# RWKV chain: state, value and right-side products with 128 weight columns, issued as two column tiles of 64

## The chip, the cores and the metric

The kernel runs on one NeuronCore of a Trainium2 chip (trn2). The metric is the device time of one execution in microseconds (us), as the median of several runs. Times of instructions, waits and the granted clock of TensorE come from one profiled execution of the kernel before the change.

Words used below: PE is TensorE's matmul stream, PEld its weight loads, DVE VectorE, ACT ScalarE, POOL GpSimd, SP the queue that issues most DMAs. A *record* is one matmul entry of the trace; each float32 matmul call of the program shows up as two records, each with its own weight load. A *tile* of the array, as in `128*64`, is the number of its rows and columns that a matmul uses.

## The reference, cut to what matters

One serving step of a two-layer hybrid model over 640 tokens (512 latent, 128 context). One of four parallel branches is an RWKV-7 time mixing with 8 heads of width 64, run forward and backward. The change touches only the scan of this branch:

```python
def rwkv7_scan(r, decay, k, v, kk, a, s0, reverse):
    def step(s, inp):
        r_t, w_t, k_t, v_t, kk_t, a_t = inp
        s_kk = jnp.einsum('bhij,bhj->bhi', s, kk_t)
        s = (s * w_t[:, :, None, :] - s_kk[..., None] * (kk_t * a_t)[:, :, None, :]
             + v_t[..., None] * k_t[:, :, None, :])
        return s, jnp.einsum('bhij,bhj->bhi', s, r_t)
    xs = tuple(jnp.moveaxis(t, 1, 0) for t in (r, decay, k, v, kk, a))
    s_fin, out = lax.scan(step, s0.astype(F32), xs, reverse=reverse)
    return jnp.moveaxis(out, 0, 1), s_fin
```

The other branches (latent attention, a Mamba-2 scan, a gated linear recurrence) and the projections around them are the same before and after.

## The kernel before, in words

Each layer begins with a large input projection (76 blocks of 128 columns). Most of its blocks are not computed at once: they stand in a queue of generators (`enqueue`, `bg`), and every stage that follows takes pieces of that queue as filler between its own instructions. A filler piece is a run of `dense` matmuls (`mm3`, L246: weights 128x128, 320 moving columns, three products per block for a split float32). The RWKV stage (`rwkv`) comes first in each layer, then attention with the linear recurrence, then the Mamba-2 scan, then merge and output.

In the RWKV stage the scan is rewritten in chunks of 64 tokens. The 8 heads are handled as 4 pairs; a pair's two heads, e = 0 and 1, lie on partitions 0-63 and 64-127 (`hs`). `rw_chain` walks through 8 steps per pair; a step takes one chunk of each direction, and in steps 0, 1, 4 and 5 also a context chunk, so it has n = 2 or 3 units. The 2 layers, 4 pairs and 8 steps make 64 steps. All float32 products of a step go through `mm` (L541):

- **c** (out `ps`, weights `Q`, moving `S`): for each unit and head, 128 rows by 64 weight columns, out on the head's half of the partitions; ACT copies it, negated, to `xs` (L832).
- **y** from the state and the values (out `ps`, weights `Q`, moving `S`, L833-836): for each head and unit, 128 rows by 128 weight columns, 64 moving columns. The accumulation starts here.
- **W xs** (out `ps`, weights `W`, moving `xs`): 64 rows by 64 columns; DVE copies the result to `un` (L844).
- **y** from the right sides (out the same `ps`, weights `W`, moving `un`, L846-848): 64 rows by 128 weight columns, 64 moving columns. The accumulation ends here.

Half of each finished y is the next state (DVE, `S`, L852), the other half the output (`on`, ACT L856 and L862, DVE L858 and L864). POOL lays the next chunk's values into `S` beforehand (L809). `rwkv` takes the steps of a chain one by one and puts pieces of the next pair's preparation (`rw_half` with the matmuls `ps<-Q,BK`, `rw_solve`, `rw_values`) and of the filler queue (`self.bg(self.rb2)`) between them.

The order on each engine is not that of the code alone. The instructions are recorded in this interleaved order and then sorted per engine by a scheduler, on its own estimates of cost, before the program is fixed; each engine then takes its list strictly as it stands, with waits on semaphores between engines.

Of the kernel before, what the change touches and what calls it, by code (L numbers as in the profile page):

```python
# [169 lines left out]
class K:  # L170
# [624 lines left out]
    def rw_chain(self, l, p, H):  # L795

        nc, pr, V, hs = self.nc, H["pr"], H["V"], self.heads2()
        on = H["on"] = p.tile([128, T], F32, name="on", tag="on", bufs=2).rearrange("p (c i) -> p c i", i=64)

        def pairs(x, s):  # L800

            return x[:, s:8 - s:7 - 2 * s] if s < 4 else x[:, s:(6 - s if s < 7 else None):7 - 2 * s]

        def state(s):

            S = [p.tile([128, 3, 64], F32, name=f"S{e}", tag=f"S{e}", bufs=2) for e in range(2)]
            for e, r in enumerate(hs):
                o = hs[1 - e]
                nc.gpsimd.tensor_copy(S[e][o, 0:2], pairs(V[o], s))  # L809
                if s in ctx:  # L810
                    nc.gpsimd.tensor_copy(S[e][o, 2], V[o, ctx[s][1]])
                if s in (0, 4):
                    nc.gpsimd.memset(S[e][r, 2], 0.0)
            return S

        ctx = {0: (1, 9), 1: (1, 8), 4: (0, 8), 5: (0, 9)}
        S = state(0)
        for e, r in enumerate(hs):
            nc.sync.dma_start(out=S[e][r, 0:2], in_=self.a["st_rw"][l, pr, r])
        for s in range(8):  # L820
            chs = [(0, s), (1, 7 - s)] + ([ctx[s]] if s in ctx else [])
            n = len(chs)
            us = []
            for d, c in chs:
                hf, u = self.unit(d, c)
                us.append((*H["half"][hf], u))
            b = self.ps("c")
            for i, (Q, W, u) in enumerate(us):
                for e, r in enumerate(hs):
                    self.mm(b[r, 64 * i:64 * i + 64], Q[e][:, u, 0], S[e][:, i])  # L830
            xs = p.tile([128, 3, 64], F32, name="xs", tag="xs", bufs=2)
            nc.scalar.activation(out=xs[:, 0:n].rearrange("p i t -> p (i t)"), in_=b[:, 0:64 * n], func=AF.Copy, scale=-1.0)  # L832
            y = self.ps("y"), self.ps("y")  # L833
            for e in range(2):
                for i, (Q, W, u) in enumerate(us):
                    self.mm(y[e][:, 64 * i:64 * i + 64], Q[e][:, u, 1:3].rearrange("p x t -> p (x t)"), S[e][:, i], i == 0, False)
            S1 = state(s + 1) if s < 7 else [p.tile([128, 3, 64], F32, name=f"S{e}", tag=f"S{e}", bufs=2) for e in range(2)]
            yield
            b = self.ps("c")
            for i, (Q, W, u) in enumerate(us):  # L840
                for r in hs:
                    self.mm(b[r, 64 * i:64 * i + 64], W[r, u, 0], xs[r, i])
            un = p.tile([128, 3, 64], F32, name="un", tag="un", bufs=2)
            nc.vector.tensor_copy(un[:, 0:n].rearrange("p i t -> p (i t)"), b[:, 0:64 * n])  # L844
            yield
            for i, (Q, W, u) in enumerate(us):  # L846
                for e, r in enumerate(hs):
                    self.mm(y[e][:, 64 * i:64 * i + 64], W[r, u, 1:3].rearrange("p x t -> p (x t)"), un[r, i], False, i == n - 1)
            v = [x[:, 0:64 * n].rearrange("p (i t) -> p i t", t=64) for x in y]
            if s < 7:  # L850
                for e, r in enumerate(hs):
                    nc.vector.tensor_tensor(out=S1[e][r, 0:n], in0=v[e][r], in1=H["fac"][r, s, 0:n].unsqueeze(2).broadcast_to([64, n, 64]), op=ALU.mult)  # L852
            for e in range(2):
                o = hs[1 - e]
                if s < 4:
                    nc.scalar.copy(pairs(on[o], s), v[e][o, 0:2])  # L856
                else:
                    nc.vector.tensor_tensor(out=pairs(on[o], s), in0=v[e][o, 0:2], in1=pairs(on[o], s), op=ALU.add)  # L858
                if s in ctx:
                    oc = on[o, ctx[s][1]]  # L860
                    if s < 4:
                        nc.scalar.copy(oc, v[e][o, 2])  # L862
                    else:
                        nc.vector.tensor_tensor(out=oc, in0=v[e][o, 2], in1=oc, op=ALU.add)  # L864
            if s in (1, 5):
                for e, r in enumerate(hs):
                    nc.sync.dma_start(out=self.a["o_rw"][l, pr, r, chs[2][0]], in_=S1[e][r, 2])
            S = S1
            yield
# [861 lines left out]
```

## Time and profile before

| | before |
|---|---|
| median of 3 runs | 2509.02 us (2506.48 to 2519.65) |
| profiled execution, its time | 2516.37 us |
| span of the profile (first to last instruction) | 2514.5 us |
| PE busy | 2393.9 us, 95% of the span |
| PEld busy | 2106.9 us, 84% |
| DVE / ACT / POOL busy | 1711.5 / 1101.0 / 512.3 us |
| mean granted TensorE clock | 0.974 |
| matmul records | 19826 |

The profiled execution took 1.9 us more than its span, and 7.35 us more than the median of the runs. Matmuls are pipelined: a record of 0.27 us may start 0.06 us after the one before it. So the busy time of one group is far more than the PE time that it takes from others, and what a group costs is read from the starts of its records and not from their lengths.

### The profile page before, as it was taken

To read this page: it belongs to the slowest core of one execution; us is meant where nothing else is said; L and a number is where in the kernel's file an instruction comes from. 1 tells how busy PE (TensorE), PEld (TensorE's weight loads), DVE (VectorE), ACT (ScalarE), POOL (GpSimd) and SP (SyncE) were. 2 spreads that over 40 slices of the span, in tenths; PEclk is the share of its full clock that TensorE was granted. 3 is DMA by queue.
4 is the path that set the end of the run, shared out by engine and by line. 5 is a ranking of instruction groups with operands and counts; after the bars stand their busy time and mean duration, and the time that the engine had idled before them with its cause. 6 is when DMAs were issued, how large, how long until landed. Compare 5 with 4: busy or idle time off the path is not lost.

```text
span 2514.5 us, 49938 instructions
## 1 busy us (share of the span) xinstructions
PE 2393.9 (95%) x19826; PEld 2106.9 (84%) x19826; DVE 1711.5 (68%) x3749; ACT 1101.0 (44%) x2178; POOL 512.3 (20%) x723
## 2 busy tenths in 40 slices
PE   6999999999998989988999999999999999999999
PEld 4887877789987878977998978797999887898799
DVE  6575666664487777589765766675637777777883
ACT  3535243433344665453335362534224456555431
POOL 0322222121101230044103130312101013103420
PEclk9999999999999999999999999898999999999999
DMA  6443333433332213633633323132224222155354
GB/s 246 149 153 98 127 112 119 126 101 101 122 130 80 86 54 123 228 111 105 212 109 127 117 76 108 60 103 67 97 81 159 94 80 91 58 190 170 115 165 134
DMA packets 159192, 300.80 MB, mean 120 GB/s; under 512 B 59880, under 2 KB 70600, under 8 KB 158960
## 3 DMA queue, kind: packets, MB, share of 16 engines
q1 hardware_dynamic: 158528, 296.24, 35.4%
q8 instruction: 156, 2.56, 0.4%
q0 software_dynamic: 432, 1.38, 0.2%
q14 instruction: 76, 0.62, 0.1%
HBM read 221.17 MB, written 76.39 MB: 118 GB/s over the span
## 4 chain that ended last, share of the span: by engine, by line
PE 71%; DVE 15%; issue 4%; ACT 4%; DMA 4%; POOL 2%; SPq 0%; DVEq 0%; POOLq 0%; ACTq 0%
PE dn L246 40%; PE ps L541 11%; PE ps L246 6%; PE pd L1173 2%; PE ps L1124 2%; PE pd L1191 2%; PE ps L192 1%; PE ps L1438 1%; PE dn L457 1%; DVE wlo L234 1%; PE pd L1036 1%; DVE lt L1465 1%; DMA u<-zd 1%; PE ps L707 1%; DVE lm L1300 1%
## 5 line engine op out<-in xcount | busy, mean ns | idle before, releaser
L246 PE MATMUL dn<-hh,whi 128*128 128x320 f32 x2368 | 765.7, 323 | 2.8 <-DVE mod L470 1.3
L246 PE MATMUL dn<-hh,wlo 128*128 128x320 f32 x2368 | 748.8, 316 | 0.0
L246 PE MATMUL dn<-hl,whi 128*128 128x320 f32 x2368 | 748.0, 316 | 0.0
L246 PEld LDWEIGHTS dn<-hh,whi 128*128 128x128 f32 x2368 | 448.2, 189 | 30.8 <-issue 9.9
L246 PEld LDWEIGHTS dn<-hh,wlo 128*128 128x128 f32 x2368 | 447.5, 189 | 11.4 <-issue 6.7
L246 PEld LDWEIGHTS dn<-hl,whi 128*128 128x128 f32 x2368 | 448.3, 189 | 9.8 <-issue 5.1
L234 DVE TENSOR_TENSOR wlo<-raw,whi 128x1024 fp32r<-128x1024 f32 (+1 forms) x184 | 244.0, 1326 | 137.2 <-ACT whi L233 135.3
L233 ACT CAST whi<-raw 128x1024 fp32r<-128x1024 f32 (+1 forms) x184 | 191.7, 1042 | 272.9 <-PE dn L246 218.6
L541 PEld LDWEIGHTS ps<-S,Q 128*128 128x128 f32 (+1 forms) x1280 | 112.6, 173 | 33.0 <-issue 20.4
L809 POOL COPY S<-V 64x128 f32<-64x128 f32 x128 | 51.9, 406 | 425.9 <-PE ps L541 297.5
L246 PE MATMUL dn<-omh,whi 128*128 128x320 f32 x400 | 131.5, 331 | 4.1 <-DVE mx L1530 4.0
L541 PE MATMUL ps<-S,Q 128*128 128x64 f32 (+1 forms) x1280 | 130.7, 267 | 3.4 <-DVE S L852 2.3
L246 PE MATMUL dn<-oml,whi 128*128 128x320 f32 x400 | 126.8, 318 | 3.5 <-DVE oml L240 3.5
L670 DVE TENSOR_TENSOR Q<-ps,cpack 64x384 f32<-64x384 f32 x160 | 88.8, 555 | 58.5 <-ACT W L668 55.2
L246 PE MATMUL dn<-omh,wlo 128*128 128x320 f32 x400 | 126.9, 318 | 0.0
L541 PE MATMUL ps<-Q,BK 64*64 64x192 f32 x1280 | 101.1, 346 | 16.6 <-DVE Q L670 14.1
L668 ACT COPY W<-ps 64x384 f32<-64x384 f32 x160 | 75.6, 472 | 83.5 <-PE ps L541 81.2
L281 ACT COPY zst<-dn 128x320 f32<-128x320 f32 (+1 forms) x104 | 43.9, 422 | 132.4 <-PE dn L246 66.7
L541 PEld LDWEIGHTS ps<-Q,BK 64*64 64x64 f32 x1280 | 62.6, 136 | 41.3 <-DVE Q L670 20.6
L277 ACT ACTIVATE zst<-dn 128x320 f32<-128x320 f32 x128 | 55.3, 434 | 86.8 <-issue 47.9
L246 PEld LDWEIGHTS dn<-omh,whi 128*128 128x128 f32 x400 | 76.8, 193 | 18.5 <-issue 8.1
L753 DVE TENSOR_TENSOR X<-X,Lu 80x31 f32<-80x31 f32 (+15 forms) x248 | 85.6, 345 | 7.1 <-DMA Lu<-lud 1.1
(572 smaller groups left out, 4929.3 us busy)
## 6 DMA issues: line engine op xcount, KB each, us to landing
raw<-in_w_in_dram SPq DMA_DIRECT2D x152, 512.0 KB
zd<-zst SPq DMA_DIRECT2D x150, 320.0 KB
raw<-in_ada_w_dram SPq DMA_DIRECT2D x48, 512.0 KB
th<-zd SPq DMA_DIRECT2D x64, 320.0 KB
raw<-in_w_branch_dram SPq DMA_DIRECT2D x32, 512.0 KB
om<-od SPq DMA_DIRECT2D x32, 320.0 KB
u<-zd SPq DMA_DIRECT2D x26, 320.0 KB
raw<-in_w_out_dram SPq DMA_DIRECT2D x16, 512.0 KB
```

What stands on the lines that cost most here:

```text
L233: nc.scalar.copy(hi[:, 0:w], raw[:, 0:w])
L234: nc.vector.tensor_tensor(out=lo[:, 0:w], in0=raw[:, 0:w], in1=hi[:, 0:w].bitcast(F32), op=ALU.subtract)
L246: self.nc.tensor.matmul(o, w[wi], x[xi][:, sl], start=first and i == 0, stop=last and i == 2)
L277: nc.scalar.activation(out=u[:, tok], in_=t, func=AF.Tanh, scale=0.5)
L541: self.nc.tensor.matmul(o, x, y, start=start, stop=stop, skip_group_check=True)
L668: nc.scalar.copy(W[r, u:u + 2].rearrange("p u x t -> p (u x t)"), ps[e][r, 0:384])
L670: nc.vector.tensor_tensor(out=Q[e][o, u:u + 2].rearrange("p u x t -> p u (x t)"), in0=ps[e][o, 0:384].rearrange("p (u x) -> p u x", u=2), ...
L753: nc.vector.tensor_tensor(out=o, in0=X[0:nb, 0:m, k:k + 1].broadcast_to([nb, m, n]), in1=Lu[0:nb, k, k + 1:].unsqueeze(1).broadcast_to([nb ...
L809: nc.gpsimd.tensor_copy(S[e][o, 0:2], pairs(V[o], s))
L1124: nc.tensor.matmul(o[64 * x:64 * x + 64], vt[:, kt, hp * 128 + 64 * x:hp * 128 + 64 * x + 64], S[hp, t, x][:, j * 128:j * 128 + 128], star ...
L1173: nc.tensor.matmul(pd[:, b, 0:w], x[:, s], y[:, sl], start=i == 0, stop=i == 2)
L1191: nc.tensor.transpose(pd[:, i // 4, i % 4 * 128:i % 4 * 128 + 128], e[:, i * 128:i * 128 + 128], self.c["ident"])
```

## The change

Both y products are issued as two calls, one for each half of the weight columns (x = 0, 1), each writing its own half of the output partitions (`h`):

```diff
@@ -833,7 +833,8 @@
             y = self.ps("y"), self.ps("y")
             for e in range(2):
                 for i, (Q, W, u) in enumerate(us):
-                    self.mm(y[e][:, 64 * i:64 * i + 64], Q[e][:, u, 1:3].rearrange("p x t -> p (x t)"), S[e][:, i], i == 0, False)
+                    for x, h in enumerate(hs):
+                        self.mm(y[e][h, 64 * i:64 * i + 64], Q[e][:, u, 1 + x], S[e][:, i], i == 0, False)
             S1 = state(s + 1) if s < 7 else [p.tile([128, 3, 64], F32, name=f"S{e}", tag=f"S{e}", bufs=2) for e in range(2)]
             yield
             b = self.ps("c")
@@ -845,7 +846,8 @@
             yield
             for i, (Q, W, u) in enumerate(us):
                 for e, r in enumerate(hs):
-                    self.mm(y[e][:, 64 * i:64 * i + 64], W[r, u, 1:3].rearrange("p x t -> p (x t)"), un[r, i], False, i == n - 1)
+                    for x, h in enumerate(hs):
+                        self.mm(y[e][h, 64 * i:64 * i + 64], W[r, u, 1 + x], un[r, i], False, i == n - 1)
             v = [x[:, 0:64 * n].rearrange("p (i t) -> p i t", t=64) for x in y]
             if s < 7:
                 for e, r in enumerate(hs):
```

The tile of the array for the state products goes from 128*128 to 128*64 (as c has it), that of the right sides from 64*128 to 64*64 (as W xs has it). The number of calls of both doubles. Nothing else in the code differs, but the scheduler sorts the whole program anew, so fillers stand at other places too.

The PE's order before, in the second step of the first pair of layer 0 (`S_2108` and `S_2109` are the states of the two heads; 64x64 is the output of a c product, 128x64 that of a y product; L246 is filler):

```order
L541 MATMUL ps<-W,Z 32x32
L541 MATMUL ps<-un,W 128x64 x2
L541 MATMUL ps<-W,Z 32x32 x19
L541 MATMUL ps<-cpack,v 64x64 x20
L541 MATMUL ps<-un,W 128x64 x4
L707 MATMUL ps<-wl,lora 128x256
L707 MATMUL ps<-al,lora 128x256
L541 MATMUL ps<-S_2108,Q_822 64x64
```

The six products of the right sides (`un,W`) of the first step stand in two groups, between pieces of the next pair's preparation, and the next step's first c product follows.

The PE's order with the change at the place that follows (the states are now called `S_2114` and `S_2115`; y products are 64x64 as well, so the last two rows of six are y):

```order
L541 MATMUL ps<-un,W 64x64 x3
L707 MATMUL ps<-wl,lora 128x384
L541 MATMUL ps<-S_2114,Q_822 64x64
...
L541 MATMUL ps<-S_2115,Q_823 64x64
L541 MATMUL ps<-S_2114,Q_822 64x64
L541 MATMUL ps<-S_2115,Q_823 64x64
L541 MATMUL ps<-S_2114,Q_822 64x64
L541 MATMUL ps<-S_2115,Q_823 64x64
L457 MATMUL dn<-raw,csil 32x256
L541 MATMUL ps<-S_2114,Q_822 64x64 x6
L541 MATMUL ps<-S_2115,Q_823 64x64 x6
L541 MATMUL ps<-xs,W 64x64 x6
```

The right sides' last products have moved behind another piece of preparation. The y products have become twelve in place of six, and they stand where they stood, between the c products and W xs; no filler follows them here before W xs does.

The PE's order with the change in the third step, n = 2 (`Q,BK` are products of the next pair's preparation):

```order
L541 MATMUL ps<-S_2317,Q_822 64x64
L541 MATMUL ps<-S_2318,Q_823 64x64
L541 MATMUL ps<-S_2317,Q_822 64x64
L541 MATMUL ps<-S_2318,Q_823 64x64
L541 MATMUL ps<-S_2317,Q_822 64x64 x4
L246 MATMUL dn<-hh,whi 128x320
L246 MATMUL dn<-hl,whi 128x320
L246 MATMUL dn<-hh,wlo 128x320
L541 MATMUL ps<-S_2318,Q_823 64x64 x4
L541 MATMUL ps<-xs,W 64x64 x4
```

Here the four y products of head 0 follow the c products directly and those of head 1 stand behind one filler triple.

## Rows read from the trace of the kernel before

**Rows 1.** The page, parts 1 and 2: busy time, and 40 slices of the span.
```profile
PE 2393.9 (95%) x19826; PEld 2106.9 (84%) x19826; DVE 1711.5 (68%) x3749; ACT 1101.0 (44%) x2178; POOL 512.3 (20%) x723
...
PEclk9999999999999999999999999898999999999999
```

**Rows 2.** Busy time of each engine in four stretches; the first and third hold the chain.
```profile
core 0: us, PE busy (x) PEld busy (x) DVE busy (x) ACT busy (x) POOL busy (x), PEclk, DMA share, GB/s
95.00:720.00 625.00, 606.29 (x5879) 520.65 (x5878) 389.95 (x926) 246.83 (x514) 126.73 (x252) 0.99 0.36 119
...
1395.00:1905.00 510.00, 499.24 (x4847) 441.88 (x4846) 315.52 (x742) 190.75 (x413) 101.53 (x218) 0.96 0.28 91
```

**Rows 3.** Who waited for whom, 95 to 1905 us: total us, times, longest.
```profile
POOL S L809 <- PE ps L541: 297.5, 60, 62.5
...
DVE un L844 <- PE ps L541: 100.2, 30, 7.4
```

**Rows 4.** PE's groups by shape: count, busy us, mean ns, idle before.
```profile
L541 PE MATMUL ps<-S,Q 128*128 128x64 f32 x640 | 94.2, 294 | 1.1 <-ACT on L862 1.1
L541 PE MATMUL ps<-un,W 64*128 64x64 f32 x640 | 53.2, 285 | 1.7 <-DVE un L844 1.7
L541 PE MATMUL ps<-S,Q 128*64 128x64 f32 x640 | 40.8, 241 | 2.3 <-DVE S L852 2.3
L541 PE MATMUL ps<-xs,W 64*64 64x64 f32 x640 | 37.2, 236 | 1.0 <-ACT xs L832 0.7
```

**Rows 5.** Timeline of PE (start us, length us): y state products, 12 and 8 records.
```profile
270.46 1.55 PE L541 MATMUL ps<-S,Q 128*128 128x64 f32 x12
271.82 0.39 PE L246 MATMUL dn<-hh,whi 128*128 128x320 f32 x1
272.05 0.30 PE L246 MATMUL dn<-hl,whi 128*128 128x320 f32 x1
...
283.88 1.10 PE L541 MATMUL ps<-S,Q 128*128 128x64 f32 x8
```

**Rows 6.** Timeline of PE: c products, 12 and 8 records.
```profile
567.20 0.57 PE L541 MATMUL ps<-S,Q 128*64 128x64 f32 x12
...
283.50 0.45 PE L541 MATMUL ps<-S,Q 128*64 128x64 f32 x8
```

**Rows 7.** Timeline of PE: right-side products, 12 and 8 records.
```profile
278.97 0.89 PE L541 MATMUL ps<-un,W 64*128 64x64 f32 x12
...
604.58 0.66 PE L541 MATMUL ps<-un,W 64*128 64x64 f32 x8
```

**Rows 8.** Timeline of PE: preparation, one head's four calls, then both heads' eight.
```profile
219.45 0.87 PE L541 MATMUL ps<-Q,BK 64*64 64x192 f32 x8
...
354.58 0.88 PE L541 MATMUL ps<-Q,BK 64*64 64x192 f32 x16
```

**Rows 9.** Timeline of PE: two kinds of 64-column products on four tiles.
```profile
349.83 0.22 PE L541 MATMUL ps<-xs,W 64*64 64x64 f32 x1
349.83 0.22 PE L541 MATMUL ps<-cpack,on 64*64 64x64 f32 x1
349.84 0.22 PE L541 MATMUL ps<-xs,W 64*64 64x64 f32 x1
349.89 0.22 PE L541 MATMUL ps<-cpack,on 64*64 64x64 f32 x1
```

**Rows 10.** Timeline of PE: from W xs to filler.
```profile
287.44 0.45 PE L541 MATMUL ps<-xs,W 64*64 64x64 f32 x8
287.82 0.42 PE L246 MATMUL dn<-hh,whi 128*128 128x320 f32 x1
288.07 0.31 PE L246 MATMUL dn<-hl,whi 128*128 128x320 f32 x1
...
278.29 0.31 PE L246 MATMUL dn<-hh,wlo 128*128 128x320 f32 x1
278.44 0.31 PE L246 MATMUL dn<-hh,whi 128*128 128x320 f32 x1
```

**Rows 11.** Two short stretches in the columns of Rows 2: before and in a fallen clock.
```profile
249.00:252.50 3.50, 1.43 (x10) 1.16 (x9) 3.47 (x5) 1.91 (x5) 3.01 (x6) 1.00 0.29 92
252.50:259.30 6.80, 6.60 (x50) 4.05 (x50) 3.05 (x6) 3.45 (x6) 3.12 (x6) 0.50 0.39 126
```

## Prediction

> **What bounds the kernel now.** I read the page first, for the engine that is busy nearly all the time: PE, 95% of the span, with DVE next at 68% and a clock that is full in nearly every slice [rows 1]. Then the four long stretches, because the change touches only the RWKV chain: it lies in two of them, 625 and 510 us long, 45% of the span. There PE is busy for 606.29 and 499.24 us, 97% and 98%; DVE, the next, for 389.95 and 315.52 us, 62% in both [rows 2]. Last the waits: other engines wait for the chain's products on PE, POOL for 297.5 us and DVE for 100.2 us [rows 3], while PE's own idle time before the four groups of the chain is 6.1 us in all, 1.1 + 1.7 + 2.3 + 1.0 [rows 4]. So in these stretches the chain does not make PE wait; PE's list of work, chain and filler together, sets their length. Whatever shortens a record's slot on PE shortens the stretch, until some other engine is late.
>
> **The price of a slot.** Busy time overlaps, so I take the difference of two groups with unequal counts, which leaves only the slots of the added records.
> - y from the state, one tile of 128*128: 12 records in 1.55 us, 8 in 1.10 us [rows 5]. (1.55 - 1.10)/4 = 0.1125 us a record.
> - c, two column tiles of 128*64, the shape that the first edit gives to y: 12 records in 0.57 us, 8 in 0.45 us [rows 6]. 0.12/4 = 0.030 us a record, so a pair, one on each column tile, takes 0.06 us. The pair loads and streams what one 128*128 record does, in half of its time.
> - y from the right sides, two row tiles of 64*128: 0.89 us for 12, 0.66 us for 8 [rows 7]. 0.0575 us a record.
> - four tiles of 64*64, the shape that the second edit gives: no row shows it alone with 64 moving columns. The preparation's products, 64*64 with 192 moving columns, show its concurrency: one head's four calls, 8 records on the two column tiles of the same 64 rows, take 0.87 us; both heads' eight calls, 16 records on all four tiles, take 0.88 us [rows 8]. The second pair of tiles is free. And where W xs and the output's transposes meet, on complementary tiles and with 64 columns each, three records start within 0.01 us and the next round 0.06 us later [rows 9]. I take half the price of two tiles, 0.030/2 = 0.015 us a record. The other bound is no concurrency beyond two tiles, 0.030 us.
>
> **The sum.** There were 640 records of each kind [rows 4]; after the change there are 1280.
> - State products: 640 x 0.1125 = 72.0 us becomes 1280 x 0.030 = 38.4 us: -33.6 us.
> - Right sides: 640 x 0.0575 = 36.8 us becomes 1280 x 0.015 = 19.2 us: -17.6 us. With the other bound it would be 38.4 us, +1.6 us.
> - Turns between tile shapes, gained: now y stands in another shape than the c in front of it. Eight c records from 283.50 end their slots at about 283.50 + 8 x 0.030 + 0.05 = 283.79 [rows 6] (0.05 for the late second record of a group), and y starts at 283.88 [rows 5]: 0.09 us, and another 0.05 us for y's own second record. After the change y simply continues c: -0.14 us, in up to 64 steps, -9 us.
> - Turns, lost: today y and filler have one shape. y's slots from 270.46 end at 270.46 + 12 x 0.1125 + 0.05 = 271.86, and the second filler record starts at 272.05 [rows 5]; less one filler slot of 0.15 (278.29 to 278.44 [rows 10]) that is 0.04 us lost. From a 64-column shape, W xs, slots end at 287.44 + 0.24 + 0.05 = 287.73 and the second filler starts at 288.07 [rows 10]: 0.19 us lost. So +0.15 us for each of some 60 changes from y to filler, +9 us. Gain and loss cancel; I set both to zero and keep 10 us either way for the range. Filler set between the two halves of a y, as in the third step shown, costs such a turn too.
> - What PE then waits: y covers ACT's copy to `xs`. A three-unit y shrinks from 12 x 0.1125 = 1.35 to 24 x 0.030 = 0.72 us, and where W xs stands directly behind it PE may reach it too early. The chain's idle time today is 6.1 us [rows 4]; I let it nearly double, +4 us. Bounds: 0, since the scheduler moves filler in between; and, if all idle time of PE in the two stretches doubled, 18.7 + 10.8 = 29.5 us [rows 2].
> - Doubled calls cost ACT, DVE, POOL and the DMA queues nothing: they have the same instructions and the same tiles; only PE's list is longer, and its cover is that PE accepts records 0.01 us apart [rows 9].
>
> Together -33.6 - 17.6 + 4 = -47 us. Against the profiled execution's 2516.37 us that is 2469 us. The median of the runs stands 7.35 us lower, at 2509.02 us: **2462 us**.
>
> **Where the Trainium skill speaks against it.** In rows 9 four records on four tiles start within 0.06 us, 0.015 us each on average. The Trainium skill, "TensorE: Matmul & The Clock Gate", section "Wait — 56ns, not 53.3ns?", states that the start-to-start time never falls below about 25 ns; by that rule the right sides' 1280 records would need 32 us, an estimate from that page, and the whole would come out some 13 us slower than forecast. The trace of this kernel does not agree, at least across tiles.
>
> **Rivals.**
> - *The right sides gain nothing*, because four tiles with such short streams run no faster than two. For it: no row shows a long run of them. Against it: rows 8 and 9. Time: 2509 - 33.6 + 1.6 + 4 = 2481 us. Chance 0.12.
> - *The freed PE time turns into waiting*, because the chain through ACT, DVE and POOL, or DVE's other work, becomes the bound. For it: y is the cover of `xs`; the scheduler orders everything anew. Against it: DVE is idle 38% of the two stretches [rows 2], and POOL and DVE wait for PE, not PE for them [rows 3, 4]. It decides if PE's idle time rises by 40 us or more, from 29.5 us to 70 us; then -51 + 40 = -11 or less, 2498 to 2512 us, no change. Chance 0.09.
> - *Column tiles do not help each other, and the kernel is slower.* If a column tile's load could not run beside a matmul of the other tile on the same rows, a 64-column record would take its load and its stream in turn. Each of them fits into the 0.06 us of a c pair [rows 6], so together at most 0.12 us. State products would cost 1280 x 0.12 = 154 us, +82; right sides, on two sets of rows, 1280 x 0.06 = 77 us, +40; 2509 + 122 = 2631 us at the most. It decides from a pair price of 0.1125 us upward. Rows 6 show 0.06 for exactly this shape, so I give it 0.03. The Trainium skill names this mechanism: the same page, section "The mechanism", has weight loads overlap with matmuls in flight only when their row groups differ, and column tiles share theirs. By that rule c could not run at 0.030 us a record; the trace disagrees.
> - *The clock falls.* In one stretch where PE was busy 1.43 of 3.50 us the granted clock was 1.00, and in the next 6.80 us it was 0.50 [rows 11], the lower of the two levels, 1.2 GHz in place of 2.4. Such a stretch loses half of its length in PE work. To eat the 47 us, 94 us more would have to run at the lower level, the means of 0.99 and 0.96 [rows 2] falling to about 0.91 and 0.87. Smaller tiles and more waits could do that; filler still fills most of the time. Then 2509 us or more. Chance 0.04.
>
> **How the numbers follow.** My forecast, both products faster and PE still the bound, has 0.72. Its own range: 47 us of gain, 10 us either way for turns, 10 us for idle time, and a few us for a clock that falls more or less often: 2444 to 2484 us. For 8 times in 10 the range takes in the case where the right sides gain nothing, with some idle time on top: **2442 to 2492 us**. A measurement of this kernel can tell about 0.5%, 12.5 us, from no change. Faster by more than that: 0.72 + 0.12 = 0.84; within it: 0.09; slower: 0.03 + 0.04 = 0.07.
>
> **What would show it.** In the profile after: the 1280 records of the state products that are no longer 128*128, 24 of them in a row in about 0.22 + 24 x 0.030 = 0.95 us beyond the c records in front; 24 right-side records in about 0.22 + 24 x 0.015 + 0.05 = 0.6 us in place of 0.89 for 12; the two chain stretches together some 45 us shorter, with PE still busy 96% or more and the other two unchanged. The forecast is wrong if those rows have these lengths and the time has not moved (then PE's waits must show where it went), or if right-side records start 0.03 us apart, or if the clock's mean in the chain stretches falls below 0.92.

## The result, and the profile after

The change made the kernel faster: 2481.22 us (median of 4 runs, 2478.02 to 2491.78) against 2513.04 us of the kernel before (4 runs, 2506.48 to 2519.65), a ratio of 0.9881 [0.9838, 0.9923]. That is 32 us, inside the range given, but two thirds of the 47 us forecast. The profiled execution took 2480.03 us, 36.3 us less than the one before.

The page of the kernel after, parts 1, 2 and 4 (busy time; granted clock in 40 slices; the chain that ended last):

```profile
span 2478.1 us, 52497 instructions
...
PE 2336.0 (94%) x21106; PEld 2053.2 (83%) x21106; DVE 1706.5 (69%) x3749; ACT 1101.4 (44%) x2178; POOL 515.6 (21%) x723
...
PEclk9999999999999999999999999999999999999999
...
PE 61%; DVE 16%; issue 4%; ACT 4%; POOL 2%; DMA 2%; SPq 0%; DVEq 0%; POOLq 0%; ACTq 0%
```

PE has 1280 records more and is busy 57.9 us less than in [rows 1]; DVE, ACT and POOL did the same work. PE's share of the span fell by only one point, because the span shrank too, but it shrank by less than the busy time did.

PE's groups of the chain and of the preparation, kernel after, by shape (count, busy us, mean ns, then the idle time before them and its releasers):

```profile
L541 PE MATMUL ps<-Q,BK 64*64 64x192 f32 x1280 | 101.8, 349 | 26.6 <-DVE Q L670 22.4 <-ACT th L708 3.9
L541 PE MATMUL ps<-S,Q 128*64 128x64 f32 x1920 | 84.2, 232 | 3.9 <-DVE S L854 2.8 <-DVE on L860 0.3 <-ACT on L864 0.3
L541 PE MATMUL ps<-un,W 64*64 64x64 f32 x1280 | 41.6, 231 | 2.3 <-DVE un L845 2.3
L541 PE MATMUL ps<-xs,W 64*64 64x64 f32 x640 | 37.5, 231 | 4.3 <-ACT xs L832 3.4 <-issue 0.9
```

The second row holds c and the new y together, 640 + 1280; the shape 128*128 of [rows 4] is gone from the chain, and so is 64*128. The waits of the chain itself stayed small: 3.9 + 2.3 + 4.3 = 10.5 us against 6.1 us. What stands out is the first row. These are products of the *next pair's preparation*, which the change does not touch. The same row of the kernel before:

```profile
L541 PE MATMUL ps<-Q,BK 64*64 64x192 f32 x1280 | 101.1, 346 | 16.6 <-DVE Q L670 14.1 <-ACT th L708 2.1
```

Its idle time grew by 10 us, and no other row of L541 by as much. The same in the waits of PE, 95 to 1905 us (total us, times, longest), first of the kernel before, then of the kernel after:

```profile
PE ps L541 <- DVE Q L670: 14.1, 15, 2.6
...
PE ps L541 <- DVE T L773: 1.9, 3, 0.6
```

```profile
PE ps L541 <- DVE Q L670: 22.4, 22, 3.3
...
PE ps L541 <- DVE T L773: 6.2, 3, 4.3
PE ps L541 <- ACT th L708: 6.1, 6, 2.2
...
PE ps L541 <- ACT xs L832: 3.4, 6, 1.0
```

`Q` L670 and `T` L773 are both DVE's, both in the preparation: L670 multiplies the preparation's products by a mask, T is the triangular solve. POOL and DVE, which waited for the chain's products on PE [rows 3], wait less now:

```profile
POOL S L809 <- PE ps L541: 218.6, 39, 24.6
...
DVE un L845 <- PE ps L541: 92.9, 28, 7.9
```

The two chain stretches of the kernel after, in the columns of [rows 2]:

```profile
core 0: us, PE busy (x) PEld busy (x) DVE busy (x) ACT busy (x) POOL busy (x), PEclk, DMA share, GB/s
95.00:695.00 600.00, 573.41 (x6453) 489.24 (x6453) 375.44 (x881) 242.54 (x507) 125.19 (x252) 0.98 0.39 122
1384.00:1872.00 488.00, 463.46 (x5475) 410.10 (x5472) 313.61 (x739) 190.35 (x411) 106.77 (x218) 0.97 0.30 94
```

The second stretch, whose ends answer to those of [rows 2], shrank by 22 us. PE's busy share fell from 97% and 98% to 96% and 95%: idle time is 600 - 573.41 = 26.6 and 488 - 463.46 = 24.5 us, 51 us in all, against 18.7 + 10.8 = 29.5 us. The clock hardly moved.

The slots themselves came out as priced. PE's timeline of the kernel after (start us, length us): state products, c and y in one row, 8 + 16 and 12 + 24 records; then right sides of three units and of two:

```profile
361.29 0.92 PE L541 MATMUL ps<-S,Q 128*64 128x64 f32 x24
...
1404.08 1.27 PE L541 MATMUL ps<-S,Q 128*64 128x64 f32 x36
```

```profile
276.50 0.58 PE L541 MATMUL ps<-un,W 64*64 64x64 f32 x24
...
300.32 0.46 PE L541 MATMUL ps<-un,W 64*64 64x64 f32 x16
```

(1.27 - 0.92)/12 = 0.029 us a record for column tiles, where 0.030 was taken from c [rows 6]. (0.58 - 0.46)/8 = 0.015 us for the right sides on four tiles, the lower of the two bounds. A whole c and y of two units took 1.48 us before (from 283.50 in [rows 6] to the end at 283.88 + 1.10 in [rows 5]) and takes 0.92 us now.

**Where the time went.** I summed the start-to-start times of consecutive records over the two chain stretches (from 95 us, and from 20 us ahead of layer 1's first c, each up to the stage's last output transposes), by what the record was. Where the next record is of another kind the time counts as a turn, and any time above 0.6 us counts as idle, with the turn that it holds. us:

| | before | after | difference | forecast |
|---|---|---|---|---|
| c and state products, slots | 92.6 | 62.9 | -29.7 | -33.6 |
| right sides, slots | 33.1 | 22.2 | -10.9 | -17.6 |
| turns between shapes | 183.0 | 165.3 | -17.7 | 0 |
| dense filler, slots | 584.4 | 588.2 | +3.8 | 0 |
| idle | 34.4 | 57.9 | +23.5 | +4 |
| all other records | 161.1 | 159.8 | -1.3 | 0 |
| total | 1088.6 | 1056.3 | -32.3 | -47 |

So PE's own work got some 56 us cheaper, more than forecast, and 23.5 us came back as idle time. About 4 us of both figures is only a change of column: there are 43 long gaps in place of 27, and each holds a usual turn of some 0.25 us that no longer counts as a turn. Of the added idle time, the long gaps at the preparation's `Q,BK` products account for 11 us: in the whole profile 10 gaps with 15.0 us beyond a usual turn of 0.25 us before, 20 with 26.2 us after. All 20 stand ahead of the first record of a group, and 11 of them ahead of the second of a half's five groups.

One such gap, kernel after. PE's timeline (start, length, and in brackets the idle time before and its releaser), then DVE's in the same 5 us:

```profile
252.06 1.22 PE L541 MATMUL ps<-Q,BK 64*64 64x192 f32 x8 [3.28 <-DVE Q L670]
```

```profile
247.64 1.47 DVE L740 TENSOR_TENSOR BK<-th,e 128x256 f32<-128x256 f32 x1
249.04 0.41 DVE L741 TENSOR_TENSOR BK<-th,e 128x256 f32<-128x256 f32 x1
249.37 1.21 DVE L234 TENSOR_TENSOR wlo<-raw,whi 128x1024 fp32r<-128x1024 f32 x1
250.50 0.91 DVE L526 SCALAR_TENSOR_TENSOR k<-s,pder,k 128x640 f32<-128x640 f32 x1
251.44 1.14 DVE L670 TENSOR_TENSOR Q<-ps,cpack 64x384 f32<-64x384 f32 x2
```

DVE is not late for want of input: it is busy without a break, on a filler block's low half (`wlo`) and a part of another branch (L526), before it reaches the mask product that PE waits for. Its list was sorted ahead of time, and PE got there first. Over the long gaps of this kind in the chain stretches DVE was busy for 93% of the waiting (94% before). Busy is not all work: the first row, 1.47 us, is an operation that takes 0.41 us elsewhere in the trace, and it ran beside one of POOL (last section).

### The profile page after: what moved, and what is told of

The parts are those of the page before. It is cut to its first block, busy times and chain, and to the rows that moved or that the text cites. A ratio compares the mean times of both kernels' runs of the same rounds, so it can differ in the third digit from the quotient of the medians.

```text
span 2478.1 us, 52497 instructions
## 1 busy us (share of the span) xinstructions
PE 2336.0 (94%) x21106; PEld 2053.2 (83%) x21106; DVE 1706.5 (69%) x3749; ACT 1101.4 (44%) x2178; POOL 515.6 (21%) x723
## 4 chain that ended last, share of the span: by engine, by line
PE 61%; DVE 16%; issue 4%; ACT 4%; POOL 2%; DMA 2%; SPq 0%; DVEq 0%; POOLq 0%; ACTq 0%
PE dn L246 35%; PE ps L541 7%; PE ps L246 5%; PE pd L1175 2%; PE ps L1126 2%; PE pd L1193 2%; DVE wlo L234 1%; PE ps L192 1%; PE ps L1440 1%; DVE lt L1467 1%; PE pd L1038 1%; PE pd L957 1%; DVE X L755 1%; DVE lm L1302 1%; DVE X L753 1%
## 5 line engine op out<-in xcount | busy, mean ns | idle before, releaser
L246 PE MATMUL dn<-hh,whi 128*128 128x320 f32 x2368 | 767.3, 324 | 3.9 <-DVE mod L470 1.5
L246 PE MATMUL dn<-hh,wlo 128*128 128x320 f32 x2368 | 748.4, 316 | 0.0
L246 PE MATMUL dn<-hl,whi 128*128 128x320 f32 x2368 | 748.1, 316 | 0.0
L246 PEld LDWEIGHTS dn<-hh,whi 128*128 128x128 f32 x2368 | 447.3, 189 | 37.0 <-issue 10.7
L246 PEld LDWEIGHTS dn<-hl,whi 128*128 128x128 f32 x2368 | 448.5, 189 | 9.9 <-issue 5.0
L246 PEld LDWEIGHTS dn<-hh,wlo 128*128 128x128 f32 x2368 | 447.6, 189 | 10.6 <-issue 6.0
L234 DVE TENSOR_TENSOR wlo<-raw,whi 128x1024 fp32r<-128x1024 f32 (+1 forms) x184 | 243.8, 1325 | 131.7 <-ACT whi L233 130.2
L246 PE MATMUL dn<-omh,whi 128*128 128x320 f32 x400 | 131.1, 330 | 1.8 <-DVE mx L1532 1.8
L246 PE MATMUL dn<-oml,whi 128*128 128x320 f32 x400 | 127.1, 319 | 3.5 <-DVE oml L240 3.5
L246 PE MATMUL dn<-omh,wlo 128*128 128x320 f32 x400 | 127.0, 319 | 0.0
L541 PE MATMUL ps<-Q,BK 64*64 64x192 f32 x1280 | 101.8, 349 | 26.6 <-DVE Q L670 22.4
L670 DVE TENSOR_TENSOR Q<-ps,cpack 64x384 f32<-64x384 f32 x160 | 88.9, 555 | 53.0 <-ACT W L668 49.1
L541 PEld LDWEIGHTS ps<-Q,BK 64*64 64x64 f32 x1280 | 64.9, 137 | 49.6 <-DVE Q L670 30.4
L541 PEld LDWEIGHTS ps<-S,Q 128*64 128x64 f32 x1920 | 70.1, 142 | 28.3 <-issue 18.3
L246 PEld LDWEIGHTS dn<-omh,whi 128*128 128x128 f32 x400 | 76.6, 193 | 16.1 <-issue 7.1
L755 DVE TENSOR_TENSOR X<-X 80x31 f32<-80x31 f32 (+15 forms) x248 | 85.2, 344 | 5.9
```

The lines of the kernel that those rows point to most:

```text
L234: nc.vector.tensor_tensor(out=lo[:, 0:w], in0=raw[:, 0:w], in1=hi[:, 0:w].bitcast(F32), op=ALU.subtract)
L246: self.nc.tensor.matmul(o, w[wi], x[xi][:, sl], start=first and i == 0, stop=last and i == 2)
L541: self.nc.tensor.matmul(o, x, y, start=start, stop=stop, skip_group_check=True)
L670: nc.vector.tensor_tensor(out=Q[e][o, u:u + 2].rearrange("p u x t -> p u (x t)"), in0=ps[e][o, 0:384].rearrange("p (u x) -> p u x", u=2), ...
L755: nc.vector.tensor_tensor(out=X[0:nb, 0:m, k + 1:], in0=X[0:nb, 0:m, k + 1:], in1=o, op=ALU.subtract)
```

## The experiments

The texts on record give the theories letters. Roughly: A, both edits save on PE and waits hand part of it back; B, the second edit saves nothing; the later letters are rivals for what makes the new waits, with E: DVE's load at the preparation is what they stand behind.

**1 and 2. Each edit alone.** e1_state has only the first hunk of the change (the state products), e2_right only the second (the right sides).

> Only the state products are split into column tiles; the right sides stay on 64*128. Theory A (slots fell as forecast, and about 20 us of it went into PE waiting for DVE in the preparation, DVE Q L670): state slots -34 us, waits +12 to +15 us, so about 20 us faster than before, ratio near 0.992, PE's wait for Q L670 over both chain stretches between 13.6 us (before) and 20.4 us (after). Theory B (the right sides on four tiles gave nothing): all of the change's 30 us is already here, ratio near 0.988.

> Only the right-side products are split; the state products stay on 128*128. Theory A: -17 us of slots, a few us of waits back, so 10 to 14 us faster, ratio near 0.995, and 24 right-side records in 0.58 us. Theory B: no change, ratio 1.000 or a little above.

Measured: the state products alone 2482.89 us (2478.85 to 2488.42), ratio 0.9886 [0.9864, 0.9909]; the right sides alone 2505.85 us, 0.9968 [0.9951, 0.9985]. Each is a gain by itself, 29.7 and 6.7 us by the medians. The sum, 36.4 us, is more than the 32 us of both in the change's own runs, but the intervals are too wide to show that from the times. The first edit alone has a ratio that cannot be told from that of the change. In the accounting above (us):

| | before | state only | right sides only | both |
|---|---|---|---|---|
| c and state products, slots | 92.6 | 60.9 | 92.4 | 62.9 |
| right sides, slots | 33.1 | 33.5 | 21.8 | 22.2 |
| turns | 183.0 | 170.4 | 178.7 | 165.3 |
| idle | 34.4 | 40.7 | 39.6 | 57.9 |
| total | 1088.6 | 1053.5 | 1081.8 | 1056.3 |

The slots add up; the turns add up (-12.6 and -4.3, together -17.7); the idle time does not: +6.3 and +5.2 alone, +23.5 together. So the right sides' saving is real on PE in both kernels that have it, and it is idle time that takes it back once the state products are cheap as well. The totals carry some clock too: the four kernels' stretches ran 61, 41, 65 and 51 us at the lower clock level. The time of e1 came out as theory B said, but e2 refutes B: its slots shrink by 11 us and its time by 7 to 8. Theory A's sizes were missed as well: it asked for 20 us of e1 and 10 to 14 us of e2.

**3 and 4. More PSUM buffers for the preparation.** If the products waited for a PSUM buffer that DVE's L670 empties, a third buffer of tag `s` should shorten the wait (the chain's c then has one in place of two). e3 on the kernel after, e4 on the kernel before.

```diff
-        eb = self.banks(f"rw{l}", s=2, c=2, y=2)
+        eb = self.banks(f"rw{l}", s=3, c=1, y=2)
```

> The changed kernel with three PSUM buffers for the small products (tag s) in place of two, and one in place of two for c and W xs (tag c), whose tiles follow each other by data anyway. Theory A with the PSUM buffers as the place: PE's wait for Q L670 falls from 20.4 us to under 8 us, and the time by 8 to 14 us more, to 2467 to 2473 us, ratio near 0.983. Theory C (PE waits because DVE has not yet made the next operands, or because the new order put less filler there): the wait stays at 15 us or more and the time stays near 2481 us.

> The same buffers in the kernel before. Theory A with the PSUM buffers as the place: the wait for Q L670 falls from 13.6 us to under 6 us, the time by 4 to 8 us, ratio near 0.9975: less than in the changed kernel, since less is lost there. Theory C: no change.

Measured: e3 2485.68 us, ratio 0.9891 [0.9868, 0.9915], not to be told from the change; e4 2536.26 us, 1.0086 [1.006, 1.0112], slower than before. PE's waits of e3 in the window of those above:

```profile
PE ps L541 <- DVE Q L670: 31.1, 30, 3.9
```

The wait rose from 22.4 to 31.1 us where it should have fallen, and in e4 from 14.1 to 19.9 us. The trace of e3 shows what the third buffer did. A group of products takes two buffers, one for each head, so a third lets only the first head's products of the next group go ahead. Of the long gaps, 13 of 25 now stand ahead of a group's ninth record, the second head's first; in the kernel after none of 20 did. At the place of the example above PE got further and then waited as long; PE's row of e3, then DVE's:

```profile
250.55 1.39 PE L541 MATMUL ps<-Q,BK 64*64 64x192 f32 x8 [3.36 <-DVE Q L670]
...
249.93 1.73 DVE L670 TENSOR_TENSOR Q<-ps,cpack 64x384 f32<-64x384 f32 x3
```

So PE does wait for a buffer that L670 empties, and one more buffer moves the wait without lifting it, since L670 itself comes late. Four buffers, enough for a whole group ahead, were not run. Why the kernel before gets slower with this edit stays open; its chain stretches ran 102 us at the lower clock level, against 61 us in the kernel before, and half of that difference is most of the 24 us.

**5. More filler in the RWKV stage**, kernel after. If PE idles because it runs out of other work there, more filler should fill the gaps.

```diff
-        k.rb2 = 1.45 if l else 1.52
+        k.rb2 = 1.62 if l else 1.69
```

> The changed kernel with 1.69 and 1.62 pieces of filler at each place of the RWKV stage in place of 1.52 and 1.45: the PE time that the change frees in a place (about 0.3 us) is filled again. Theory C (DVE's list of work is late for the preparation, and PE waits at its products): more filler between them gives DVE time, PE's wait for Q L670 falls from 22.4 us to under 15 us and the time by 5 to 12 us, to 2469 to 2476 us. Theory D (the loss lies in the newly sorted list, by chance, and not in a shortage of filler): no consistent change, 2475 to 2490 us, and the wait stays at 18 us or more.

Measured: 2499.08 us, 0.9927 [0.9899, 0.9955], some 18 us slower than the change by the medians (the intervals of the two ratios overlap); the wait for L670 25.9 us. The time lies outside both theories' bands; the wait rose, as D allows and C does not. The RWKV stretches got 27 and 18 us longer, the stages behind them only some 20 and 5 us shorter. Most of the added filler does not land in the gaps: idle time in the accounting is 52.7 us against 57.9. That each block brings its own `wlo` for DVE (L234 in the timeline above), the engine PE waits for, may be why; no run separates this.

**6. The order of the right sides' calls**, kernel after: the two heads (different rows) inside, the two halves (different columns) outside.

```diff
             for i, (Q, W, u) in enumerate(us):
-                for e, r in enumerate(hs):
-                    for x, h in enumerate(hs):
+                for x, h in enumerate(hs):
+                    for e, r in enumerate(hs):
```

> The changed kernel with the two inner loops of the right-side products exchanged (the column half outside, the head inside): the same calls on the same four tiles, in another order within a group of four, so the same slots; only the sorting can differ. Theory D: the time moves by 8 us or more either way, since the list differs. Theory C: it stays within 5 us of 2481 us.

Measured: 2477.39 us, 0.9833 [0.9758, 0.9908]; the wait for L670 24.0 us. The time is within 5 us of 2481 us, as C said, and the interval overlaps that of the change. The order of the four tiles is not where the missing gain is, and idle time in the accounting is 57.2 us with this other list, against 57.9.

**7 and 8. DVE relieved, POOL loaded.** In the RWKV stage the low halves `wlo` of the filler's weights are made by POOL in place of DVE; e7 on the kernel after, e8 on the kernel before.

```diff
-        nc.vector.tensor_tensor(out=lo[:, 0:w], in0=raw[:, 0:w], in1=hi[:, 0:w].bitcast(F32), op=ALU.subtract)
+        (nc.gpsimd if self.lop else nc.vector).tensor_tensor(out=lo[:, 0:w], in0=raw[:, 0:w], in1=hi[:, 0:w].bitcast(F32), op=ALU.subtract)
...
+        k.lop = True
         k.rwkv(l, od[0])
+        k.lop = False
```

> The changed kernel with the filler weights' low part (wlo, 1.33 us a piece on DVE) subtracted on POOL during the RWKV stage: about 80 pieces, 105 us of DVE work less in the two chain stretches, some 200 us more on POOL, which is busy about a fifth of the time. Theory C: PE's wait for Q L670 falls from 22.4 us to under 14 us, and the time by 5 to 12 us, to 2469 to 2476 us. Theory D: no fall of the wait, time within 5 us of 2481 us; if POOL hands the weights over too late, PE waits for wlo instead and the time rises.

> The same move of wlo to POOL in the kernel before. Theory C: less to gain, since PE waited 14.1 us there: 2 to 6 us faster, 2507 to 2511 us. Theory D: no change; if POOL is late, slower.

Measured: e7 2566.99 us, 1.0188 [1.0122, 1.0253]; e8 2601.25 us, 1.0322 [1.0257, 1.0388]. Both are slower, and the change is still worth 34 us between them, about what it is without the edit. The profile of e7 shows why this relieves nothing. Its groups by line, 95 to 1905 us, POOL's `wlo` and one of DVE's; then DVE's row in the kernel after, same window (it is a line lower in e7):

```profile
L235 POOL TENSOR_TENSOR wlo<-raw,whi 128x1024 fp32r<-128x1024 f32 x87 | 211.6, 2433 | 373.0 <-ACT whi L234 341.1 <-DVE S L855 19.1 <-PE dn L247 5.0
...
L754 DVE TENSOR_TENSOR X<-X,Lu 80x31 f32<-80x31 f32 (+15 forms) x248 | 114.6, 462 | 12.3 <-DMA Lu<-lud 5.9
```

```profile
L753 DVE TENSOR_TENSOR X<-X,Lu 80x31 f32<-80x31 f32 (+15 forms) x248 | 83.7, 338 | 9.0 <-DMA Lu<-lud 3.0
```

The 248 steps of the solve, same shapes and same count, take 462 in place of 338 ns each on average. DVE lost the `wlo` and got slower at the rest, where it ran beside POOL's (last section): this pair says nothing on a DVE with less to do.

**9, 10 and 11. DVE relieved, ACT loaded.** Two of the preparation's products on DVE become copies on ACT: e9 on the kernel after, e10 on the kernel before, e11 on the kernel with the state products alone.

```diff
-        tt(out=Ro, in0=ch(H["r"][:, sl]), in1=A[:, :, incl], op=ALU.mult)
+        nc.scalar.copy(Ro, ch(H["r"][:, sl]))
...
-        tt(out=BK[:, :, 1], in0=ch(kd), in1=B[:, :, incl], op=ALU.mult)
+        nc.scalar.copy(BK[:, :, 1], ch(kd))
```

> The changed kernel with two of the four products that prepare a half chain (L739 and L741, 38 us of DVE in the two chain stretches) replaced by plain copies on ACT; the multiplication by the decay is left out there. Theory E (DVE is busy without a pause at these places and PE reaches them too early, so the freed time is lost there until DVE is done): PE's long waits at the preparation fall from 26 us to 12 to 18 us and the time to 2462 to 2472 us. Theory D (the loss is an accident of the newly sorted list): no particular fall of these waits, time within 5 us of 2481 us.

> The same replacement in the kernel before. Theory E: PE waits there for 15 us only, so it falls less, to 2505 to 2510 us, and the change is worth more between these two kernels than between the original ones: 36 to 45 us in place of 30. Theory D: the two differ by 30 us or less.

> The same replacement with only the state products split. Original kernels: with the right sides split as well, nothing was gained beyond this. Theory E: with DVE relieved the right sides' slots (-11 us) are worth something again, and this run is 5 to 11 us slower than the changed kernel with the replacement. Theory B (the right sides on four tiles give nothing once the state products are split): the two are within 3 us.

Measured: e9 2476.98 us, 0.984 [0.9818, 0.9863]; e10 2510.47 us, 0.9988 [0.9971, 1.0006]; e11 2481.22 us, 0.9857 [0.9835, 0.9878]. With DVE relieved the change is worth 33.5 us (e10 less e9), below the 36 to 45 us that theory E asked for and above the 30 us of its rival; the second edit on top of the first is worth 4.2 us (e11 less e9), also between the two bands. The time of e9 itself lies in D's band, within 5 us of 2481 us, and not in E's. PE's wait for L670 fell from 22.4 to 18.8 us in e9 and did not move in e10 (14.5 for 14.1) nor in e11 (17.4 for 17.1). The long gaps at `Q,BK` fell from 26.2 to 21.8 us in e9, where E asked for 12 to 18. Idle time in the accounting fell in all three, from 57.9 to 47.9 us in e9, 34.4 to 27.1 in e10 and 40.7 to 35.9 in e11. The direction is that of E, the size is not; intervals of half a per cent cannot carry more.

**12. Another place for the preparation's breaks**, kernel after. A half's five groups are recorded with a break after units 2 and 6; with breaks after 0 and 4, the second group, at which most gaps stand, is recorded behind a break.

```diff
-            if u in (2, 6):
+            if u in (0, 4):
```

> The changed kernel with the breaks in a half's preparation products moved: the five groups stand as 1, 2, 2 in place of 2, 2, 1, so chain and filler come between the first group and the second. In the changed kernel's trace 12 of PE's 20 long waits at these products stand before the second group, whose buffers DVE has still to empty behind a backlog. Theory E (PE comes too early, right behind a DVE backlog): the long waits at these products fall from 26 us to 18 us or less, the time by 4 to 10 us, to 2471 to 2477 us. Theory D (accident of the sorted list): the waits stay at 22 us or more, the time anywhere within 10 us of 2481 us.

Measured: 2475.23 us (2469.03 to 2477.88, 6 runs), 0.9833 [0.9801, 0.9866]. The long gaps at `Q,BK` fell from 26.2 to 23.4 us, not to the 18 expected. PE's waits of e12, window as above:

```profile
PE ps L541 <- DVE Q L670: 19.4, 23, 2.5
```

The longest wait fell from 3.3 to 2.5 us, the number stayed. The time lies in both theories' bands and the gaps in D's. This kernel has the lowest median of the study, but its interval still overlaps that of the change, so it is not shown to be better. Nothing that was tried beats it by more.

**All lists together.** Theory D, an accident of one sorted list, can be held against every trace, since each kernel was sorted anew. Idle time in the accounting is 57.9, 57.2 (e6), 55.4 (e12), 52.7 (e5), 52.3 (e3) and 47.9 us (e9) in the six kernels with both edits, and 40.7 (e1), 40.3 (e4), 39.6 (e2), 35.9 (e11), 34.4 (before) and 27.1 us (e10) in the six with one edit or none; e7 and e8, which load POOL, are left out. The two sets do not meet, one profiled execution each, so an accident of a single list does not explain it. Between kernels that differ by the whole change it grows by 23.5 us, by 20.8 us (e10 to e9) and, with the third buffer, by 12.0 us (e4 to e3).

## Why the prediction was right in sign and range, and 15 us too far

- **PE's list sets the length of the two stretches: held.** The 36.3 us between the two profiled executions lie nearly all in them (32.3 us by the accounting above).
- **State products, -33.6 us: right.** 0.029 us a record measured in long rows against 0.030 taken; the slots fell by 29.7 us (c and y together).
- **Right sides, -17.6 us: the price right, the sum too large.** 0.015 us a record was the lower bound and is what long rows show. But the sum priced 1280 records as if they stood in long rows. Many stand in pieces between products of the preparation, as the second listing of the change shows in its first rows, and a piece ends with a turn: there were 73 pieces before and 107 after. Starts lie 0.016 us apart in the 43 whole rows of 16 or 24 and 0.028 us in the 36 pieces of 2 to 11 records, 0.019 on average. Slots fell by 10.9 us in the change and by 11.3 us alone (e2). The rival that the right sides gain nothing gave 2481 us, the measured time, by a wrong road: e2 gains 7 to 8 us.
- **Turns, set to zero: too cautious.** They fell by 17.7 us. The two traces split it. The gain of y continuing c was there: 62 turns from c to y cost 9.8 us before, and after the change those starts are ordinary slots, some 2 us. The loss at the end of y was smaller than its 9 us: 54 turns from y to filler cost 5.8 us before and 58 cost 9.3 us after, +3.4 us. Some 4 us went to the idle column, as said above, and the turns from right sides to filler fell from 10.8 to 8.4 us. The rest is spread. The clock is not in it: turns at the lower level took 10.8 us before and 10.4 us after.
- **What PE then waits, +4 us: this is the step that failed.** It asked where PE could wait *in the chain*, and there it was right, 6.1 to 10.5 us. But from "DVE is idle 38% of the two stretches" [rows 2] it took DVE's other work as no likely bound. An average does not show this: in the gap above DVE had some 4 us of work standing in a row, and the preparation's mask product stood behind it. Idle time rose by 23.5 us (19.5 without the turns that it took over), within the bound of 29.5 us named for it and far from the value taken. The row that would have shown the place was there before, with the largest idle time of all of L541: `Q,BK`, 16.6 us. The prediction read only the chain's four. That the whole still came out inside the range owes something to the turns, whose unforecast gain made up for most of this.
- **The rival that freed time turns into waiting** was half right. It was to decide from 70 us of idle time; 51 us were reached.
- **The rule against the change.** A start-to-start time of at least about 25 ns, which the Trainium skill states ("TensorE: Matmul & The Clock Gate", section "Wait — 56ns, not 53.3ns?"), would have made eight more records cost at least 8 x 0.025 = 0.20 us, an estimate from that page. The two rows of right sides above show 0.12 us: across four tiles the rule does not hold.
- **Column tiles do not help each other, and the clock falls**: neither happened. 0.029 us a record, and a mean clock of 0.979 against 0.974. The clock rival's sum was off: 94 us more at half speed in 1135 us lower the mean by 0.04, to about 0.95 and 0.92, not to 0.91 and 0.87.

**Shown**: the prices of the slots, that they add up, that idle time does not, and that it is longer in each of six lists with both edits than in any of six with fewer; that about half of the added idle time stands at the preparation's products, with DVE busy for 93% of it, and that PE waits there for a buffer which DVE's L670 empties (e3). **Open**: why the idle time grows by more with both edits than with the two alone. That PE with less work simply comes too early for DVE fits all of this, but DVE's load and the order in which its list takes its work were not separated: e9 and e12 moved the wait for L670 by 3 to 4 us, e10 and e11 not at all. The other half of the added idle time is spread over `T`, `th`, `xs` and small gaps, and was not traced to one cause.

## What to carry to other kernels

Price a slot from two groups of unequal count: the difference of their lengths was right to 0.001 us here, while the right sides' busy time in the change, 41.6 us, is nearly twice the 22.2 us of their slots. A product with few moving columns (64 here) was cheaper as more, smaller tiles, most of all where its records stood together. When an engine that is 97% busy gets 50 us less to do, look beyond the rows that the change touches: read what that engine waits for already, at all of its groups, since that wait is what grows.

## What the runs showed of the hardware

- **Four tiles share PE finely.** Eight more right-side records cost 0.12 us on four tiles, where the four wider ones that did the same work on two row tiles cost 4 x 0.0575 = 0.23 us [rows 7].
- **A DVE operation that begins beside one of POOL can be held until that one ends.** The mean of 462 ns in e7 hides two kinds: of the 248 operations of L754, the 16 that began while POOL's `wlo` ran took 2180 ns on average, the 198 that began beside nothing on POOL 336 ns. One of POOL's rows in e7 and two of DVE's around it, of nearly the same size:

```profile
180.03 2.59 POOL L235 TENSOR_TENSOR wlo<-raw,whi 128x1024 fp32r<-128x1024 f32 x1 [5.79 <-ACT whi L234]
...
179.47 0.42 DVE L754 TENSOR_TENSOR X<-X,Lu 80x255 f32<-80x255 f32 x1
...
180.38 2.51 DVE L754 TENSOR_TENSOR X<-X,Lu 80x252 f32<-80x252 f32 x1
```

  The long one ends 0.27 us after POOL's. In the kernel after it is the same with L740 and L741 in the timeline above, 1.47 and 0.41 us for one size: L740 began beside this row and ended 0.28 us after it, L741 ran beside POOL copies of two columns only.

```profile
247.51 1.32 POOL L523 TENSOR_TENSOR s<-u 128x638 f32<-128x638 f32 x1
```

  Not every operation is held: L670, which reads PSUM, took 555 ns with POOL idle and 554 ns beside it (kernel after). In the chain stretches 30 DVE operations before and 36 after ran over 0.15 us longer than the median of their shape beside an idle POOL, 24.6 and 30.7 us in all, and every one of them began while POOL ran something. So a part of DVE's busy time in these stretches is waiting for POOL; no run took it away.
- **POOL needs 2433 ns** for a 128x1024 subtraction of float32 (e7); the group of DVE's `wlo` has a mean of 1326 ns in the kernel before.
